# Four token-major projection blocks of 256 columns joined into two pairs of 512

## The chip, the cores and the metric

The kernel runs on one core of a Trainium2 chip. The metric is the device time of one execution in microseconds (us), as the median of several runs. The profile comes from one further execution of the same program.

## The reference, cut to what matters

The program is one transformer layer over 512 + 1024 tokens of width 1024, in fp32. The part at issue is the input projection and what consumes it:

```
u    = rmsnorm(x) * g                      # 1536 tokens x 1024
proj = u @ w_in + b_in                     # split by columns:
       na_q, na_k, na_v   512 each         # neighbourhood attention
       gla_q, gla_k       256 each         # gated linear attention (GLA)
       gla_v, gla_g       512 each
       lr_fwd, lr_bwd      16 each         # decay gates of the GLA
       gate_na, gate_gla 1024 each
gla  = bidirectional scan(gla_q, gla_k, gla_v, decay), normed, * silu(gla_g)
```

The kernel keeps each fp32 operand as a high and a low part and forms a product from three matmuls: high by high, high by low, low by high. A "split" makes the two parts: ScalarE (ACT) copies with rounding to the high part, VectorE (DVE) subtracts it from the source for the low part.

## The kernel before, in words

The token operand (`u_hi`, `u_lo`) stays in SBUF. The projection runs as a list of units. **Channel-major units** (`dense_cm`, line 211) hold a weight tile of 128 columns stationary and stream 512 tokens: 8 steps of three matmuls of 512 columns (lines 225 to 227). **Token-major units** (`dense_tm`, line 255, with `tm_half`, line 244) hold 128 tokens stationary and stream a weight block of 256 columns: 8 steps of three matmuls of 256 columns (lines 250 to 252). There are six token-major blocks of 256 columns: 0 and 1 are `gla_v`, 2 and 3 `na_v`, 4 and 5 `gla_g`. Block 0 is done earlier with the gate columns; the middle stage does the others, twelve token tiles each, the last two tiles together in one unit.

The order of the middle stage is the list `mid` (line 815): block 4, the channel-major `k1`, blocks 1, 5, 2, 3, then eight channel-major `na` tiles and eight gate units. `run_dense` (line 343) walks this list. Each step yields a cost (0.325 for a token-major step, 0.65 for a channel-major one), and when the summed cost passes 3.9 the generator `gla_all` (line 554) issues its next piece. So the GLA is laid between the projection's matmuls by hand, every 12 steps of 256 columns or every 6 of 512. Engines run their instructions in the order in which they are issued.

The GLA treats 512 tokens at a time in eight **levels**. A level is a group of score matmuls on PE (line 622), then on DVE `ew` (line 625) for the next level's operands and `merge`, which copies the scores out of PSUM (on ACT for the last two levels). Two PSUM banks hold scores, so the next score group waits for the merges of this one. After the last segment of a sequence come an update of the states, three pieces of `scan` (line 710: 24 DVE operations for the longer sequence) and the outputs (`out_mm`, line 718), which need the finished scan.

Evictions: when a token tile is done, `out_tm` (line 313) is issued within the next two steps. DVE adds the bias into a staging tile `st` (two buffers). Blocks 4 and 5 then go through ACT (Silu) and GpSimd and a store. Blocks 2 and 3 are split by ACT and DVE into a tile `svr` or `svl` (one buffer each, by turns) and stored by two DMAs. All DMAs here are issued by SyncE (SP) in order.

Weights pass a ring (`Ring`, line 32): two raw buffers, and three pairs of high and low, each with its own fixed place; all are 128 x 1024. An item is half a 256-column block, or one channel-major tile. PSUM gives three banks to projection results.

Of the kernel before, what the change touches and what calls it, by code (L numbers as in the profile page):

```python
# [31 lines left out]
class Ring:  # L32


    def __init__(self, nc, raw, rawtag, nraw, pool, tag, nslots, items):
        self.nc, self.raw, self.pool, self.items = nc, raw, pool, items
        self.rawtag, self.tag, self.nraw, self.nslots = rawtag, tag, nraw, nslots
        self.loaded, self.parts = [], []

    def load(self):  # L40
        i = len(self.loaded)
        t = self.raw.tile([128, 1024], F32, tag=self.rawtag, bufs=self.nraw, name=f"{self.tag}r{i}")
        self.nc.sync.dma_start(t, self.items[i])
        self.loaded.append(t)

    def split(self):
        i = len(self.parts)
        t = self.loaded[i]
        hi = self.pool.tile([128, 1024], F32R, tag=self.tag + "h", bufs=self.nslots, name=f"{self.tag}h{i}")
        lo = self.pool.tile([128, 1024], F32R, tag=self.tag + "l", bufs=self.nslots, name=f"{self.tag}l{i}")  # L50
        self.nc.scalar.activation(hi, t, AF.Copy)  # L51
        self.nc.vector.tensor_tensor(lo, t, hi.bitcast(F32), op=ALU.subtract)  # L52
        self.parts.append((hi, lo))

    def fill(self, live):

        n = len(self.items)
        while True:
            if len(self.loaded) < n and len(self.loaded) - len(self.parts) < self.nraw:
                self.load()  # L60
            elif len(self.parts) < len(self.loaded) and len(self.parts) - live < self.nslots:
                self.split()
            else:
                return

    def step(self, live):

        if len(self.parts) < min(len(self.items), live + self.nslots):
            if len(self.loaded) == len(self.parts):
                self.load()  # L70
            self.split()
            if len(self.loaded) < len(self.items):
                self.load()

    def get(self, i):
        return self.parts[i]
# [3 lines left out]
def tile_trunk(ctx: ExitStack, tc: tile.TileContext, d: dict, y: bass.AP):  # L80
    nc = tc.nc
# [25 lines left out]
    rngp = rnge.enter_context(tc.tile_pool(name="rng", bufs=1))  # L107
# [22 lines left out]
    def add_mv(b):  # L130
        add(f"mv{b}", d["wmv"][2 * b], d["wmv"][2 * b + 1])
# [17 lines left out]
    ring = Ring(nc, raw, "wraw", 2, rngp, "w", 3, items)  # L149
# [8 lines left out]
    zero = cst.tile([128, 128], F32, name="zero")  # L158
    V.memset(zero, 0.0)
# [78 lines left out]
    TM = (0, 4, 1, 5, 2, 3)  # L238

    def load_brow(b):  # L240
        brow[b] = stg2.tile([128, 256], F32, tag="brow", name=f"brow{b}")
# [13 lines left out]
    def dense_tm(b, i, evac):  # L255
# [4 lines left out]
        def mm():  # L260
            if i == 0:
                ring.fill(wi)
            if b not in brow:
                load_brow(b)
            if i == 6 and TM.index(b) < 5:
                load_brow(TM[TM.index(b) + 1])
# [11 lines left out]
        return mm  # L278

# [33 lines left out]
    def out_tm(p, b, i):  # L313
# [108 lines left out]
    def norm_side():  # L422
# [11 lines left out]
        gkw = p0.tile([128, 512], F32, name="gkw")  # L434
# [30 lines left out]
        for i in range(1, 12):  # L465
# [6 lines left out]
            if i == 4:  # L472
                SP.dma_start(gkw, d["gkw"])
                load_brow(4)
                SP.dma_start(gng, d["gng"])
# [10 lines left out]
    ns = norm_side()  # L486
    warm = ps("b")
# [1366 lines left out]
```

## Time and profile before

| | |
|---|---|
| median of 3 runs | 2114.01 us (2112.49 to 2114.92) |
| profiled execution, its own time | 2115.74 us |
| its span, first to last instruction | 2114.1 us |
| PE (TensorE matmuls) busy | 2097.4 us, 99% |
| DVE busy | 1320.2 us, 62% |
| ACT busy | 974.5 us, 46% |
| granted TensorE clock, mean | 0.998 |

The span is the first instruction's start to the last one's end. Matmuls overlap one another, so the busy time of PE says only that it had work; its pace is the distance between two starts. "PEclk" is the granted clock as a share of 2.4 GHz.

### The profile page before, as it was taken

How to read it: one execution, taken by the hardware profiler on the slowest of the kernel's cores; microseconds unless marked ns; L12 is line 12 of the kernel's file. 1: busy time of each engine (PE TensorE's matmuls, PEld its weight loads, DVE VectorE, ACT ScalarE, POOL GpSimd, SP SyncE). 2: the span in 40 equal slices, each digit the busy share in tenths (PEclk: the TensorE clock that was granted, in tenths of full speed). 3: DMA queues.
4: the chain of work that ended last, by engine and by line, in shares of the span. 5: the costliest groups of instructions: out<-in, count | busy, mean ns of one | idle time of the engine just before them, and what ended most of it. 6: DMA issues, size and time to landing. Idle time of an engine off the chain costs nothing.

```text
span 2114.1 us, 32007 instructions
## 1 busy us (share of the span) xinstructions
PE 2097.4 (99%) x11964; PEld 1890.3 (89%) x11964; DVE 1320.2 (62%) x2428; ACT 974.5 (46%) x1914; POOL 66.8 (3%) x92
## 2 busy tenths in 40 slices
PE   9999999999999999999999999999999999999998
PEld 8899998887888888898898999999999888888887
DVE  6465885767346666465476777997887444443543
ACT  6532232333345555452353666676666333233442
POOL 1020200000000000000000000000000000000000
PEclk9999999999999999999999999999999999999999
DMA  6342334464376776466666566766876755454643
GB/s 210 115 151 83 97 112 143 122 168 92 110 243 201 222 213 202 148 212 227 239 219 248 175 162 174 227 202 197 264 236 176 261 200 188 155 169 165 219 170 110
DMA packets 256426, 381.86 MB, mean 181 GB/s; under 512 B 35856, under 2 KB 163856, under 8 KB 256272
## 3 DMA queue, kind: packets, MB, share of 16 engines
q1 hardware_dynamic: 256128, 379.56, 57.4%
q8 instruction: 94, 1.54, 0.3%
q14 instruction: 60, 0.49, 0.1%
q10 hardware_dynamic: 144, 0.26, 0.0%
HBM read 256.02 MB, written 123.73 MB: 180 GB/s over the span
## 4 chain that ended last, share of the span: by engine, by line
PE 81%; DVE 2%; DMA 1%; ACT 1%; issue 1%; POOLq 0%; SPq 0%; DVEq 0%; ACTq 0%
PE psd L225 6%; PE psd L227 6%; PE psd L226 6%; PE psa L1416 4%; PE psa L1417 4%; PE psa L1418 4%; PE psa L1571 2%; PE psa L1572 2%; PE psa L1570 2%; PE psb L1571 2%; PE psb L1570 2%; PE psb L1572 2%; PE psc L1571 2%; PE psc L1572 2%; PE psc L1570 2%; PE psc L976 2%
## 5 line engine op out<-in xcount | busy, mean ns | idle before, releaser
L154 DVE TENSOR_TENSOR al<-al,ah 128x1024 fp32r<-128x1024 f32 x82 | 100.2, 1223 | 146.4 <-ACT ah L153 139.2
L153 ACT ACTIVATE ah<-al 128x1024 fp32r<-128x1024 f32 x82 | 86.6, 1058 | 226.3 <-DMA al<-ads 134.3
L225 PE MATMUL psd<-uhiS,wh 128*128 128x512 f32 x448 | 180.3, 402 | 0.8 <-ACT st L287 0.8
L227 PE MATMUL psd<-uhiS,wl 128*128 128x512 f32 x448 | 175.4, 391 | 0.0
L226 PE MATMUL psd<-uloS,wh 128*128 128x512 f32 x448 | 174.9, 390 | 0.0
L1416 PE MATMUL psa<-c,uwh 128*128 128x384 f32 x512 | 171.8, 335 | 1.4 <-ACT xa L1363 0.8
L1417 PE MATMUL psa<-c,uwh 128*128 128x384 f32 x512 | 171.1, 334 | 0.1
L1418 PE MATMUL psa<-c,uwl 128*128 128x384 f32 x512 | 171.0, 334 | 0.0
L1321 DVE TENSOR_TENSOR uwl<-ux,uwh 128x512 fp32r<-128x512 f32 x192 | 131.1, 687 | 59.3 <-ACT uwh L1337 58.4
L52 DVE TENSOR_TENSOR wl<-wr,wh 128x1024 fp32r<-128x1024 f32 x70 | 85.5, 1223 | 115.0 <-ACT wh L51 104.1
L1337 ACT ACTIVATE uwh<-ux 128x512 fp32r<-128x512 f32 x192 | 119.9, 625 | 80.1 <-DVE ux L1331 66.7
L51 ACT ACTIVATE wh<-wr 128x1024 fp32r<-128x1024 f32 x70 | 73.8, 1055 | 146.6 <-PE psc L1221 66.0
L225 PEld LDWEIGHTS psd<-uhiS,wh 128*128 128x128 f32 x448 | 84.2, 188 | 19.2 <-ACT st L287 1.2
L227 PEld LDWEIGHTS psd<-uhiS,wl 128*128 128x128 f32 x448 | 84.1, 188 | 18.3
L226 PEld LDWEIGHTS psd<-uloS,wh 128*128 128x128 f32 x448 | 84.3, 188 | 16.0
L1416 PEld LDWEIGHTS psa<-c,uwh 128*128 128x128 f32 x512 | 96.1, 188 | 2.1 <-ACT xa L1363 1.1
L1417 PEld LDWEIGHTS psa<-c,uwh 128*128 128x128 f32 x512 | 96.1, 188 | 0.5 <-DVE c L1271 0.4
L1418 PEld LDWEIGHTS psa<-c,uwl 128*128 128x128 f32 x512 | 96.1, 188 | 0.0
L250 PE MATMUL psd<-wh,uhiS 128*128 128x256 f32 x320 | 93.2, 291 | 0.0
L225 PE MATMUL psd<-uhiP,wh 128*128 128x512 f32 x224 | 90.8, 405 | 0.0
L251 PE MATMUL psd<-wl,uhiS 128*128 128x256 f32 x320 | 90.8, 284 | 0.0
L252 PE MATMUL psd<-wh,uloS 128*128 128x256 f32 x320 | 90.7, 283 | 0.0
(547 smaller groups left out, 5897.7 us busy)
## 6 DMA issues: line engine op xcount, KB each, us to landing
ux<-in_wup_dram SPq DMA_DIRECT2D x64, 512.0 KB
al<-ads SPq DMA_DIRECT2D x48, 512.0 KB
al<-ad SPq DMA_DIRECT2D x34, 512.0 KB
bq<-t_d SPq DMA_DIRECT2D x64, 256.0 KB
wr<-in_wst_dram SPq DMA_DIRECT2D x28, 512.0 KB
gate_d<-st SPq DMA_DIRECT2D x48, 256.0 KB
sg<-gate_d SPq DMA_DIRECT2D x32, 384.0 KB
ad<-xa SPq DMA_DIRECT2D x64, 192.0 KB
```

Of the source, the lines that this page charges most:

```text
L154: V.tensor_tensor(lo, src, hi.bitcast(F32), op=ALU.subtract)
L225: T.matmul(p, wh, xh[:, k, sl], start=(k == 0), stop=False)
L226: T.matmul(p, wh, xl[:, k, sl], start=False, stop=False)
L227: T.matmul(p, wl, xh[:, k, sl], start=False, stop=(k == 7))
L1321: V.tensor_tensor(lo, usrc.pop(m - 1), hi.bitcast(F32), op=ALU.subtract)
L1337: A.activation(uhl[m][0], usrc[m], AF.Copy)
L1416: T.matmul(u[b], wh[:, es], c[:, 0, k], start=(new and k == 0), stop=False, skip_group_check=True)
L1417: T.matmul(u[b], wh[:, es], c[:, 1, k], start=False, stop=False, skip_group_check=True)
L1418: T.matmul(u[b], wl[:, es], c[:, 0, k], start=False, stop=(k == 3), skip_group_check=True)
L1570: T.matmul(p, ah[:, jj], bh[:, cs], start=((new or last) and jj == 0), stop=False, skip_group_check=True)
L1571: T.matmul(p, ah[:, jj], bl[:, cs], start=False, stop=False, skip_group_check=True)
L1572: T.matmul(p, al[:, jj], bh[:, cs], start=False, stop=(kh == 1 and jj == 7), skip_group_check=True)
```

## The change

The blocks (4, 5) and (2, 3) become two pairs. A pair has one weight tile for each of its 8 steps, `[128, 1024]`, high part in the left 512 columns and low part in the right; a step is three matmuls of 512 columns, and a pair needs 8 steps for a token tile where its two blocks needed 16 of half the width. The first unit takes token tiles 0 and 1 together, the last one 10 and 11. The weights of a pair come as eight raw tiles of 128 x 512, loaded into the tiles `svr` and `svl`, two at a time. The ring's eight buffers of 128 x 1024 serve raw, high or low as they come free, and also hold the eight tiles of a pair. `k1` is moved to the front, block 1 to the end. Pair 0's weights are split during `k1`, pair 1's during pair 0's last unit, block 1's during pair 1's last unit.

```diff
 class Ring:
-    def __init__(self, nc, raw, rawtag, nraw, pool, tag, nslots, items):
...
+    def __init__(self, nc, pool, nbuf, items):
+        self.nc, self.pool, self.items = nc, pool, items
+        self.free, self.limit, self.done = list(range(nbuf)), len(items), 0
         self.loaded, self.parts = [], []
+    def alloc(self, dt, name):
+        s = self.free.pop(0)
+        return s, self.pool.tile([128, 1024], dt, tag=f"w{s}", name=name)
...
+    def release(self, live):
+        while self.done < min(live, len(self.parts)):
+            self.free += self.parts[self.done][:2]
+            self.done += 1
...
-    for n in ("q0", "k0", "q1"):
+    for n in ("q0", "k0", "q1", "k1"):
         add(n, d["wst"][ST[n]])
-    add_mv(4)
-    add("k1", d["wst"][3])
-    add_mv(1)
-    add_mv(5)
-    add_mv(2)
-    add_mv(3)
+    add("mv1", d["wmv"][0], d["wmv"][1])
...
-    ring = Ring(nc, raw, "wraw", 2, rngp, "w", 3, items)
+    ring = Ring(nc, raw, 8, items)
+    ring.limit = where["mv1"]
-    zero = cst.tile([128, 128], F32, name="zero")
-    V.memset(zero, 0.0)
...
+    PAIRS = ((4, 5), (2, 3))
+    pw = [dict(n=0, raw=[], parts={}) for _ in PAIRS]
+    def pw_step(q, split=True):
+        w = pw[q]
+        if split and w["raw"] and ring.free:
+            k = len(w["parts"])
+            t = w["raw"].pop(0)
+            s, x = ring.alloc(F32R, f"pw{q}{k}")
+            split_act(x[:, :512], x[:, 512:], t)
+            w["parts"][k] = s, x
+        while w["n"] < 8 and len(w["raw"]) < 2:
+            t = stg2.tile([128, 512], F32, tag=("svr", "svl")[w["n"] % 2], bufs=1, name=f"pr{q}{w['n']}")
+            SP.dma_start(t, d["wpr"][q, w["n"]])
+            w["raw"].append(t)
+            w["n"] += 1
+    def pw_ahead(mm, q):
+        def run():
+            for n, cost in enumerate(mm()):
+                yield cost
+                if n % 3 == 2:
+                    pw_step(q)
+        return run
+    def dense_pair(q, i, evac, nxt=None):
+        def step(p, k, j):
+            x = pw[q]["parts"][k][1]
+            xh, xl = tok_ap(u_hi, k, j), tok_ap(u_lo, k, j)
+            T.matmul(p, xh, x[:, :512], start=(k == 0), stop=False)
+            T.matmul(p, xh, x[:, 512:], start=False, stop=False)
+            T.matmul(p, xl, x[:, :512], start=False, stop=(k == 7))
+        def end(p, j):
+            for e in range(2):
+                evac(p[:, e * 256:e * 256 + 256], PAIRS[q][e], j)
+        def mm():
+            if i == 0 and q == 0:
+                ring.release(where["k1"] + 1)
+            if i == 9 and nxt:
+                nxt(-1)
+            ii = (i, i + 1) if i in (0, 10) else (i,)
+            p = {}
+            for k in range(8):
+                for _ in range(2):
+                    if k not in pw[q]["parts"]:
+                        pw_step(q)
+                for j in ii:
+                    if k == 0:
+                        if j == 1:
+                            flush()
+                        p[j] = ps("d")
+                    step(p[j], k, j)
+                    yield 0.68
+                    if k == 7:
+                        done.append(lambda j=j: end(p[j], j))
+                if i == 0:
+                    pw_step(q)
...
+                if i == 10:
+                    ring.free.append(pw[q]["parts"][k][0])
+                    if nxt:
+                        nxt(k)
+        return mm
+    def next_pair(k):
+        pw_step(1, k >= 0)
+    def next_ring(k):
+        ring.limit = len(items)
+        if k in (0, 1):
+            ring.load()
+        elif k in (3, 5):
+            ring.split()
...
-            r = stg2.tile([128, 4, 2, 64], F32R, tag=("svr", "svl")[i % 2], bufs=1, name=f"svr{uid[0]}")
+            r = stg2.tile([128, 4, 2, 64], F32R, tag=("svr", "svl")[(i + b) % 2], bufs=1, name=f"svr{uid[0]}")
...
-    mid = []
-    mid += [dense_tm(4, i, out_tm) for i in range(12)]
-    for n_, dst, cb in (("k1", glak_d, 3),):
-        mid += [dense_cm(n_, seg, out_cm(dst, cb, 128, cb < 2)) for seg in range(3)]
-    for b in (1, 5, 2, 3):
-        mid += [dense_tm(b, i, out_tm) for i in range(12)]
+    mid = [pw_ahead(dense_cm("k1", seg, out_cm(glak_d, 3, 128)), 0) for seg in range(3)]
+    for q, nxt in enumerate((next_pair, next_ring)):
+        mid += [dense_pair(q, i, out_tm, nxt) for i in (0, *range(2, 11))]
+    mid += [dense_tm(1, i, out_tm) for i in range(12)]
```

The bias rows of a pair are loaded earlier (three buffers in place of two), the zeros for the warm-up matmuls share a buffer with another tile and are written a little later, and the later stages take their weight buffers from the same eight in the same number as before.

## Rows read from the trace of the kernel before

**Rows 1.** By stretch: busy us (instructions) of each engine, then granted clock, DMA share, GB/s.

```profile
core 0: us, PE busy (x) PEld busy (x) DVE busy (x) ACT busy (x) POOL busy (x), PEclk, DMA share, GB/s
112.00:222.00 110.00, 110.00 (x880) 103.02 (x879) 65.83 (x123) 30.90 (x67) 14.67 (x18) 1.00 0.38 121
...
267.00:328.00 61.00, 60.57 (x531) 58.46 (x530) 49.49 (x105) 16.82 (x38) 0.73 (x1) 1.00 0.34 109
...
332.00:336.00 4.00, 4.00 (x21) 3.83 (x20) 1.08 (x3) 0.42 (x1) 0.00 (x0) 0.57 0.20 60
```

**Rows 2.** Line 250: instructions by form, duration ns min/median/max, first and last start.

```profile
L250 PE MATMUL psd<-wh,uhiS x320: 278/283/561, 127.1 to 358.8; 128*128 128x256 f32 x160
...
L250 PE MATMUL psd<-wh,uhiP x160: 277/283/386, 115.6 to 323.8; 128*128 128x256 f32 x160
```

**Rows 3.** Timeline of PE, 256-column products: start, duration, engine, line (56 starts apart).

```profile
204.94 0.28 PE L250 MATMUL psd<-wh,uhiS 128*128 128x256 f32 x1
...
211.66 0.28 PE L252 MATMUL psd<-wh,uloS 128*128 128x256 f32 x1
```

**Rows 4.** Timeline of PE, last stage, 512-column products (31 starts apart).

```profile
1719.84 0.39 PE L1571 MATMUL psa<-bl,ah 128*128 128x512 f32 x1
...
1726.86 0.39 PE L1572 MATMUL psb<-bh,al 128*128 128x512 f32 x1
```

**Rows 5.** Timeline of DVE, block 2: a level begins, the next eviction, the one after.

```profile
277.20 0.69 DVE L633 TENSOR_TENSOR Q0S<-q0S,Y0S 128x512 f32<-128x512 f32 x1
...
281.17 0.41 DVE L316 TENSOR_TENSOR sv<-psd,brow 128x256 f32<-128x256 f32 x1
...
282.46 0.42 DVE L316 TENSOR_TENSOR sv<-psd,brow 128x256 f32<-128x256 f32 x1
```

**Rows 6.** Chain of waits ahead of the long wait of PE: start, duration, what.

```profile
318.63 4.09 DMA nv_d<-svr
...
322.83 0.42 ACT svr L153
```

**Rows 7.** Timeline of PE at that wait; in brackets the idle time and its end.

```profile
331.62 0.46 PE L727 MATMUL psb<-stt0S,qd0S 128*128 128x128 f32 x2 [2.57 <-DVE stt0S L716]
```

**Rows 8.** Chain of waits, 512-column section: two score groups, one level apart.

```profile
369.72 1.09 PE psa L622 x16
...
375.12 0.97 PE psa L622 x13
```

**Rows 9.** Timeline of DVE, block 4: two evictions through the same staging buffer.

```profile
119.53 0.42 DVE L316 TENSOR_TENSOR sv<-psd,brow 128x256 f32<-128x256 f32 x1
...
125.63 0.42 DVE L316 TENSOR_TENSOR sv<-psd,brow 128x256 f32<-128x256 f32 x1 [3.66 <-DMA glag_d<-sv]
```

**Rows 10.** Timeline of SP, same stretch: the store between them.

```profile
121.24 0.32 SPq L335 DMA_DIRECT2D glag_d<-sv  x1
```

**Rows 11.** The page, part 5: splits of 512 elements.

```profile
L1321 DVE TENSOR_TENSOR uwl<-ux,uwh 128x512 fp32r<-128x512 f32 x192 | 131.1, 687 | 59.3 <-ACT uwh L1337 58.4
...
L1337 ACT ACTIVATE uwh<-ux 128x512 fp32r<-128x512 f32 x192 | 119.9, 625 | 80.1 <-DVE ux L1331 66.7
```

**Rows 12.** Timelines of SP and DVE: a 256 KB load, and the instruction that its landing released.

```profile
930.58 0.32 SPq L1072 DMA_DIRECT2D xr<-go_d  x1
...
933.33 1.23 DVE L52 TENSOR_TENSOR wl<-wr,wh 128x1024 fp32r<-128x1024 f32 x1 [0.26 <-DMA xr<-go_d]
```

**Rows 13.** Timelines of SP and ACT: a 512 KB load, and the split that it released.

```profile
62.16 0.33 SPq L43 DMA_DIRECT2D wr<-in_wst_dram  x1
...
65.81 1.06 ACT L51 ACTIVATE wh<-wr 128x1024 fp32r<-128x1024 f32 x1 [6.19 <-DMA wr<-in_wst_dram]
```

**Rows 14.** Timeline of DVE: scaled queries, then the first scan of eight operations.

```profile
308.47 0.68 DVE L683 TENSOR_TENSOR qd0S<-q0S,Y0S 64x512 f32<-64x512 f32 x1
...
319.19 0.34 DVE L715 SCALAR_TENSOR_TENSOR stt0S<-stt0S,cd0S 64x128 f32<-64x128 f32 x1
...
322.22 0.42 DVE L316 TENSOR_TENSOR sv<-psd,brow 128x256 f32<-128x256 f32 x1
```

**Rows 15.** Timeline of PE, first products after the warm-up.

```profile
8.45 1.09 PE L193 MATMUL psa<-ident,xn 128*128 128x128 f32 x8 [1.39 <-DVE xn L185]
```

More of the change, by code (lines that the diff above doesn't have):

```diff
@@ L64, in fill @@
                 return
[L66 to L73, printed above, removed]
     def get(self, i):
-        return self.parts[i]
+        return self.parts[i][2:]
 @with_exitstack
@@ L262, in mm @@
                 ring.fill(wi)
[L263 to L266, printed above, removed]
             if i == 11:
@@ new lines, in pw_ahead @@
+    def pw_ahead(mm, q):
[37 more added lines that the diff above has]
+                    pw_step(q)
+                    if k == 4:
+                        for b in PAIRS[q]:
+                            if b not in brow:
+                                load_brow(b)
+                if i == 6 and k == 0:
+                    load_brow(PAIRS[1][0] if q == 0 else 1)
+                if i == 10:
[3 more added lines that the diff above has]
+        return mm
@@ L433, in norm_side @@
         SP.dma_start(gkb, d["gkb"])
-        gkw = p0.tile([128, 512], F32, name="gkw")
         xn = {}
@@ L472, in norm_side @@
             if i == 4:
+                gkw = p0.tile([128, 512], F32, tag="v0r", bufs=2, name="gkw")
                 SP.dma_start(gkw, d["gkw"])
                 load_brow(4)
+                load_brow(5)
                 SP.dma_start(gng, d["gng"])
@@ L486, in tile_trunk @@
     ns = norm_side()
+    zero = p0.tile([128, 4, 32], F32, tag="lrt", bufs=4, name="zero").rearrange("p a b -> p (a b)")
+    V.memset(zero, 0.0)
     warm = ps("b")
@@ L1224, in wout @@
                         V.tensor_tensor(hs, acc[t], hs, op=ALU.add)
+                ring.release(wi + 1)
                 hook(n * 4 + kq)
@@ L1290, in factors @@
         return out
-    uraw, uhl, useq = {}, {}, []
+    uraw, uhl, useq, uslot = {}, {}, [], {}
     for p in range(33):
@@ L1300, in u_load @@
             for e in es:
-                x = raw.tile([128, 1024], F32, tag="wraw", bufs=2, name=f"ux{p}{e}") if p % 2 == 0 else tmp(f"ux{p}{e}")
+                s, x = ring.alloc(F32, f"ux{p}{e}") if p % 2 == 0 else (None, tmp(f"ux{p}{e}"))
+                uslot.setdefault(p, []).append(s)
                 SP.dma_start(x, d["wup"][p % 16 * 2 + e])
@@ L1324, in u_step @@
                 uraw.pop(p)
+                ring.free += [s for s in uslot.pop(p) if s is not None]
                 u_load(p + 2)
@@ L1333, in u_step @@
             if m % 2 == 0:
-                uhl["t"] = [rngp.tile([128, 1024], F32R, tag=f"w{c}", bufs=3, name=f"uw{c}{m}") for c in "hl"]
+                uslot["w", m + 1], uhl["t"] = zip(*[ring.alloc(F32R, f"uw{c}{m}") for c in "hl"])
             sl = slice(m % 2 * 512, m % 2 * 512 + 512)
@@ L1418, in up_all @@
                         T.matmul(u[b], wl[:, es], c[:, 0, k], start=False, stop=(k == 3), skip_group_check=True)
+                    ring.free += uslot.pop(("w", n), ())
                     ev(pos)
@@ L1778, in _layout @@
     mv = [gv, gv + 256, nav, nav + 256, gg, gg + 256]
-    d["wmv"] = c(np.stack([stat(w[h * 512:(h + 1) * 512, m:m + 256]) for m in mv for h in range(2)]))
+    d["wmv"] = c(np.stack([stat(w[h * 512:(h + 1) * 512, gv + 256:gv + 512]) for h in range(2)]))
+    d["wpr"] = c(np.stack([w[:, m:m + 512].reshape(8, 128, 512) for m in (gg, nav)]))
     v0 = np.concatenate([w[:, gv:gv + 256], w[:, lr:lr + 32]], 1)
```

27 lines of the change are left out of this document (10 added, 17 removed).

## The prediction

> **What bounds the kernel now.** I read the shares of the engines first: PE is busy 99% of the span, so what counts is its pace and the few places where it has nothing to do. The windows by stage come next [rows 1]. From 112 to 222 us PE never rests and DVE is at 60%; from 267 to 328 us, under blocks 2 and 3, DVE is busy 81% of the time and PE loses 0.43 us. Just after comes the longest wait of the middle stage, and in the window behind it the granted clock is 0.57, so part of it is at 1.2 GHz: 4 x 0.43 = 1.7 us lost. Line 250 shows 480 matmuls [rows 2], 96 for each of five blocks; lines 251 and 252 repeat them, so the four joined blocks have 4 x 96 x 3 = 1152. Their start-to-start distance is (211.66 - 204.94)/56 = 0.120 us [rows 3]. For a streamed operand of 512 columns, tokens stationary, the last stage shows (1726.86 - 1719.84)/31 = 0.2265 us [rows 4].
>
> The second bound stands close behind. In block 2 one level occupies DVE from 277.20 to 281.17, 3.97 us, and one eviction 1.29 us, because the subtraction waits in line for ACT's copy [rows 5]. A level of PE is 36 x 0.120 + 1.3 = 5.6 us and holds 1.5 evictions, so DVE needs 3.97 + 1.94 = 5.9: DVE, not PE, sets the pace there. The chain ahead of the long wait says the same: a store of `svr` holds ACT's next copy 4.20 us, from 318.63 to 322.83 [rows 6], the scan stands behind it on DVE, and PE waits 2.57 us for the scan [rows 7].
>
> **What the matmuls give.** 1152 x 0.120 = 138.2 us become 576 x 0.2265 = 130.5: -7.8 us, all on PE. The Trainium skill, "TensorE: Matmul & The Clock Gate", section on the 56 ns gap, has N/2.4 GHz plus about 2.5 ns between warm matmuls; by that the joining would give only about 1.5 us and the kernel would end some 6 us later than I say. The trace does not agree with it: 13 ns, not 2.5, lie on top of 256/2.4 = 107.
>
> **What the shorter time asks of DVE.** Score groups in a 512-column section are 375.12 - 369.72 = 5.40 us apart [rows 8]: six steps of 3 x 0.2265 (4.08) and 1.3. Pairs cost 0.68 a step, so 3.9/0.68 = 5.74 steps, 3.9 us, lie between two pieces: 5.2 us a level. DVE's work per token is unchanged, but the evictions now come in twos, and in fours at the first and last unit of a pair, where two token tiles end one step apart. The staging buffers are still two, `svr` and `svl` one each. A staging buffer of blocks 4 and 5 came back 6.1 us after its eviction (119.53 to 125.63 [rows 9]), 4.39 of them after SP issued the store [rows 10]. Four places follow, with t the start of a score group; the group after the next needs the work of the level between.
>
> *A, tokens 0 and 1 of pair 0.* The third and fourth eviction must wait for the first two buffers. Token 0 ends at t + 3.3; buffers back at t + 9.4 and 9.8; last eviction ends at t + 10.3, the level behind it at t + 14.2. PE wants it at t + 10.4. Wait 3.8.
>
> *B, from pair 0 to pair 1.* Eight splits of 512, about 0.69 each on DVE and 0.63 on ACT [rows 11], must run in the last unit, with only two raw buffers. A 256 KB load took 2.75 us from issue to use [rows 12], a 512 KB one 3.65 [rows 13]; I take 3.2, between the two, since SP also carries stores here. A buffer's round is 3.2 + 0.63 + 0.69 = 4.5. From the unit's start: splits end at 2.7, 4.0, 7.2, 8.5, 11.7; a level's 3.97 stands behind the fifth (15.7); 16.4, 17.1; token 10's evictions 17.9; the eighth split 20.9; token 11's evictions wait for buffers, 17.1 + 6.1 = 23.2, and end at 24.1; the next level at 28.1. PE wants that after 22 steps (15.0) and three pieces of GLA (3.4), at 18.4. Wait 9.7, on PE in several parts.
>
> *C, tokens 0 and 1 of pair 1.* Token 0 ends 8.6 us after the last score group of B; its evictions 9.9 and 11.2. Token 1's first copy waits for `svr`, 9.9 + 4.2 = 14.1, its second for `svl`, 15.4; they end at 16.3, the level behind at 20.3. PE wants it at 3 x 5.2 = 15.7. Wait 4.6.
>
> *D, levels 2 to 5 under the rest of pair 1.* 0.72 token per level, 2 x 1.29 each: DVE needs 3.97 + 1.85 = 5.8 against 5.2. Wait 4 x 0.6 = 2.4.
>
> *E, from pair 1 to block 1.* The scan now falls into the last unit and behind it. Between the state update and the outputs DVE has scaled queries (1.4), two splits of 1024 (2.5, at the 1.23 of [rows 12]), 24 scan operations (3 x 3.03 = 9.1 [rows 14]), four evictions (5.2), a wait for `svr` (4.2 - 1.3 = 2.9) and a light eviction (0.4): 21.4 us. PE has 3.9 x 3.9 = 15.2. Wait 6.2. The same sum for before, 20.6 against 16.8, gives 3.8 where 2.57 was seen, so it is good to about 1 us.
>
> Together 26.7 us of new waits. What goes: the old waits and the slow clock behind them, 0.43 + 2.57 + 1.7 = 4.7. What comes with the new: before, PE had waited 2.57 us ahead of the fall of the clock. B, C and E have waits of that size and A too; PE running slowly lets DVE catch up, so I count three of the four, 3 x 1.7 = 5.1.
>
> **What costs nothing.** k1's place: pair 0's first five splits run under k1's 16 us of matmuls, where ACT is mostly idle (30.9 of 110 us); if late, PE waits a split, 1.3 us. Each pair loads eight times 256 KB in place of four times 512 KB: 8 more issues of 0.32 us on SP, which waits more than it issues. GpSimd's 24 multiplications are the same. The later zeros for the warm-up hide in the 1.39 us that PE waits after it [rows 15]; uncovered, some tenths. Later stages get the same buffers in the same order.
>
> **Sum:** -7.8 - 4.7 + 26.7 + 5.1 = +19.3 us. The profiled execution's own 2115.7 us (span 2114.1) becomes 2135.0; it stands 1.7 us above the median, which becomes 2114.0 + 19.3 = 2133.3.
>
> **Rivals.**
> *Faster, the buffers come back in time.* If staging and raw buffers return within about 2 us, the queue of DVE alone counts: A and B fit, C keeps 2.0, D 0.4 (the before, too, lost only 0.43), E 18.5 - 15.2 = 3.3. Then -7.8 - 4.7 + 5.7 = -6.8: 2107 us. For it speaks the 512-column section, where PE keeps 5.40; against it both returns of over 4 us. 0.17.
> *Half the waits.* Returns of some 2.2 us and loads of 1.6: A 1.7, B 4.2, C 2.6, D 1.4, E 4.2, one slow clock: +3.3, 2117 us. 0.13. By the Trainium skill, "DMA: Bandwidth & Descriptors", section on the anatomy of one DMA (there for DMAs that GpSimd issues), a transfer takes 2.0 us plus its bytes over 436 GB/s, 2.3 us for these stores, which would be this case; the rows, with SP issuing, show 4.2 and 4.4.
> *More.* Loads of 3.65, four slow clocks, E's store issues in a row before the return counts, k1's cover gone: +5 to +8, about 2140 us. 0.20.
> *The pair's matmuls are not faster than two halves.* Nothing gained, 2141 us; rows 4 have the same shape of operands. 0.02.
>
> **The numbers.** My forecast has 0.48 and the price of a load or a return moves it between 2124 and 2138. A measurement of this kernel tells about 0.2% (4.2 us) from no change. Faster by more: the first rival and a little of the second, 0.18. Within: part of the second and the forecast's edge, 0.08. Slower: 0.74. The range leaves out the first rival and the top: 2110 to 2149.
>
> **What would show it.** Right: 576 starts 0.227 apart; PE waits for DVE merges (line 660), or for the eviction's bias addition, at the four places; DVE waits of 3 to 4 us ended by stores of `sv` and `svr`; windows with a clock below 1; the scan wait longer than 2.57. Wrong: score groups 5.2 us apart through both pairs, or evictions of token 1 that wait for no store.

## The result and the profile after

| | before | after |
|---|---|---|
| median of the runs | 2114.21 us | 2152.34 us (2152.24 to 2153.85) |
| ratio, 95% interval | | 1.0182 (1.017 to 1.0194) |
| profiled execution, own time / span | 2115.74 / 2114.1 us | 2152.37 / 2150.6 us |
| granted clock, mean | 0.998 | 0.990 |

Slower by 38.1 us; the forecast was 19.3, the range ended at 2149. From the page of the kernel after:

```profile
span 2150.6 us, 30885 instructions
PE 2105.2 (98%) x11388; PEld 1868.8 (87%) x11388; DVE 1320.4 (61%) x2436; ACT 976.2 (45%) x1922; POOL 64.7 (3%) x92
...
PEclk9999899999999999999999999999999999999999
```

DVE and ACT have the same work as before, to 2 us. To see where the time went, each distance between two starts of matmuls is taken apart: PE's idle time, half of the rest where the granted clock is at its lower level (1.2 of 2.4 GHz), and what is left, PE's streaming at full clock. Summed over the span:

| us | before | after | difference |
|---|---|---|---|
| PE idle | 9.2 | 37.9 | +28.7 |
| lost at the lower clock | 3.4 | 15.3 | +11.9 |
| streaming | 2093.7 | 2089.7 | -4.1 |

The sum, +36.5, is the difference of the spans. The stretch at the lower clock in the first 30 us, ahead of the middle stage, differs from trace to trace: 1.7 us of before's 3.4 stand there, none of after's 15.3. From 420 us on the two kernels idle alike; the loss lies in the middle stage. This is what PE waits for from 100 to 420 us (engine, bank and line of the matmul, then the releaser; total, times, longest), to be read against [rows 7]:

```profile
PE psa L694 <- DVE att0S L732: 16.0, 4, 5.4
PE psd L239 <- DVE sv L385: 6.4, 1, 6.4
PE psa L694 <- DVE att0P L732: 4.4, 1, 4.4
PE psd L240 <- DVE wl L54: 2.5, 1, 2.5
PE psa L683 <- issue: 1.9, 1, 1.9
```

Lines 694 and 732 are the scores and the merge (622 and 660 of before), 239 and 240 block 1's matmuls, 385 the eviction's bias addition, 683 the first level of GLA. The matmuls ahead of the waits start at 130.3 (1.87 us), 154.6 (4.44: place A), 225.4 and 237.9 (5.41 and 4.87: B), 261.4 (5.32: C), 341.9 and 350.3 (2.48 and 6.40: E); D lost 1.4 in small pieces. Behind each large one PE ran at the lower clock. The windows behind A, both waits of B, C and E, in the columns of [rows 1]:

```profile
160.00:166.00 6.00, 5.97 (x29) 4.96 (x30) 5.93 (x11) 0.75 (x2) 1.25 (x2) 0.72 0.00 0
...
230.00:235.00 5.00, 3.77 (x19) 3.24 (x20) 3.62 (x7) 1.38 (x3) 1.13 (x2) 0.50 0.83 260
...
243.00:250.00 7.00, 6.89 (x28) 5.71 (x29) 6.87 (x14) 0.00 (x0) 0.00 (x0) 0.57 0.02 7
...
266.00:273.00 7.00, 5.93 (x24) 4.92 (x25) 5.55 (x11) 2.78 (x9) 0.00 (x0) 0.51 0.07 23
...
355.00:362.00 7.00, 5.00 (x24) 5.03 (x25) 5.67 (x17) 0.83 (x2) 0.00 (x0) 0.52 0.50 145
```

Between them PE keeps its pace. Two starts from the timeline of PE, fifteen matmuls apart (other lines left out):

```profile
301.12 0.39 PE L298 MATMUL psd<-pw,uhiS 128*128 128x512 f32 x1
...
304.54 0.39 PE L298 MATMUL psd<-pw,uhiS 128*128 128x512 f32 x1
```

(304.54 - 301.12)/15 = 0.228 us, as [rows 4] had it. Why PE waits is told by the queues of DVE, ACT and SP (timeline: start, length, engine and line; in brackets the idle time before and what ended it), in the order A (four), C (two), and four at E:

```profile
148.26 0.76 DVE L385 TENSOR_TENSOR sv<-psd,brow 128x256 f32<-128x256 f32 x2 [0.92 <-PE psd L299]
...
148.76 1.28 ACT L401 ACT_TABLE_LOAD   x1 [7.98 <-DVE sv L385]
...
151.35 6.39 SPq L404 DMA_DIRECT2D glag_d<-sv  x4
...
154.15 0.93 DVE L385 TENSOR_TENSOR sv<-psd,brow 128x256 f32<-128x256 f32 x2 [5.13 <-DMA glag_d<-sv]
...
261.54 0.42 ACT L145 ACTIVATE svr<-sv 128x256 fp32r<-128x256 f32 x1 [4.27 <-DMA nv_d<-svr]
262.78 0.42 ACT L145 ACTIVATE svr<-sv 128x256 fp32r<-128x256 f32 x1 [0.82 <-DVE sv L385]
...
348.52 7.06 SPq L47 DMA_DIRECT2D wr<-in_wst_dram  x3
...
352.91 1.06 ACT L53 ACTIVATE wh<-wr 128x1024 fp32r<-128x1024 f32 x1 [6.24 <-DMA wr<-in_wst_dram]
...
354.00 1.23 DVE L54 TENSOR_TENSOR wl<-wr,wh 128x1024 fp32r<-128x1024 f32 x1 [6.87 <-ACT wh L53]
...
357.68 0.34 DVE L787 SCALAR_TENSOR_TENSOR stt0S<-stt0S,cd0S 64x128 f32<-64x128 f32 x1
```

At A, DVE stands 5.13 us before a bias addition, for a store that must give a staging buffer back; the next level is behind it in DVE's queue. At C, ACT stands for a store of `svr` (the trace gives the tiles `svr` and `svl` this one name). It is the tile filled last: an eviction takes `svr` or `svl` by `(i + b) % 2`, so the last eviction of a token and the first of the next one share a tile. At E, na0's weights are loaded and split at once: DVE stands 6.87 us before that split, ahead of the third and the fourth eviction and the scan. For B, the chain that ended last, from 216 us on (start, length, what; a DMA from its issue):

```profile
217.13 2.67 DMA pr<-in_wpr_dram
...
220.55 0.70 DVE pw L146
221.27 5.11 DMA pr<-in_wpr_dram
...
226.46 0.64 ACT pw L145
...
227.12 0.70 DVE pw L146
...
258.55 2.83 DMA nv_d<-svr
```

The first raw load takes 2.67 us, the third 5.11: 3 us before it the 1 MB of `v0S` went out. The last line is at C: the store that ACT waits for.

### The profile page after: what moved, and what is told of

It is laid out like the page before. It is cut to its first block, busy times and chain, and to the rows that moved or that the text cites. A ratio compares the mean times of both kernels' runs of the same rounds, so it can differ in the third digit from the quotient of the medians.

```text
span 2150.6 us, 30885 instructions
## 1 busy us (share of the span) xinstructions
PE 2105.2 (98%) x11388; PEld 1868.8 (87%) x11388; DVE 1320.4 (61%) x2436; ACT 976.2 (45%) x1922; POOL 64.7 (3%) x92
## 4 chain that ended last, share of the span: by engine, by line
PE 86%; DVE 5%; DMA 3%; issue 3%; ACT 2%; POOL 1%; SPq 0%; POOLq 0%; ACTq 0%; DVEq 0%
PE psd L215 7%; PE psd L217 7%; PE psd L216 7%; PE psa L1489 4%; PE psa L1490 4%; PE psa L1491 4%; PE psa L1646 2%; PE psa L1644 2%; PE psa L1645 2%; PE psb L1644 2%; PE psb L1646 2%; PE psb L1645 2%; PE psc L1646 2%; PE psc L1644 2%; PE psc L1645 2%
## 5 line engine op out<-in xcount | busy, mean ns | idle before, releaser
L54 DVE TENSOR_TENSOR wl<-wr,wh 128x1024 fp32r<-128x1024 f32 x62 | 75.8, 1224 | 132.6 <-ACT wh L53 110.3
L53 ACT ACTIVATE wh<-wr 128x1024 fp32r<-128x1024 f32 x62 | 65.3, 1055 | 141.5 <-PE psc L1291 65.0
L217 PE MATMUL psd<-uhiP,wl 128*128 128x512 f32 x224 | 87.7, 392 | 0.0
L216 PE MATMUL psd<-uloP,wh 128*128 128x512 f32 x224 | 87.4, 390 | 0.0
L1491 PE MATMUL psb<-c,uwl 128*128 128x384 f32 x256 | 85.5, 334 | 0.0
```

The lines of the kernel that those rows point to most:

```text
L216: T.matmul(p, wh, xl[:, k, sl], start=False, stop=False)
L217: T.matmul(p, wl, xh[:, k, sl], start=False, stop=(k == 7))
L1491: T.matmul(u[b], wl[:, es], c[:, 0, k], start=False, stop=(k == 3), skip_group_check=True)
```

## The experiments

"Idle" and "slow" are the sums of the table above, for each run's own profile. Each ratio is to the kernel before on the same chip. A profile is one execution: those of x3_fill5, y4_abce and v4_half took 2.8 to 3.5 us more than their medians, and of the slow clock up to 3.3 us lie in the first 30 us (1.7 in x4_half, 3.3 in z3_ring).

| run | median us | ratio, 95% | idle | slow |
|---|---|---|---|---|
| changed kernel | 2152.34 | 1.0182 (1.0170 to 1.0194) | 37.9 | 15.3 |
| x1_pack | 2144.80 | 1.0144 (1.0129 to 1.0159) | 35.4 | 7.8 |
| x2_vlate | 2150.19 | 1.0171 (1.0154 to 1.0188) | 35.0 | 15.2 |
| x3_fill5 | 2148.43 | 1.0163 (1.0148 to 1.0178) | 35.9 | 15.3 |
| x5_rawq | 2153.73 | 1.0186 (1.0171 to 1.0201) | 36.9 | 18.5 |
| x4_half | 2153.11 | 1.0184 (1.0169 to 1.0199) | 35.5 | 11.8 |
| y1_abc | 2134.59 | 1.0098 (1.0083 to 1.0113) | 25.6 | 8.8 |
| y2_fill | 2150.47 | 1.0174 (1.0159 to 1.0189) | 24.0 | 10.8 |
| y4_abce | 2129.78 | 1.0072 (1.0055 to 1.0089) | 21.2 | 13.4 |
| z1_single | 2141.50 | 1.0127 (1.0112 to 1.0142) | 30.8 | 13.7 |
| z2_order | 2132.21 | 1.0081 (1.0064 to 1.0097) | 23.8 | 10.1 |
| z3_ring | 2118.62 | 1.0022 (1.0012 to 1.0031) | 11.3 | 5.0 |
| z5_lazy | 2129.48 | 1.0067 (1.0050 to 1.0084) | 21.8 | 6.4 |
| v1_inpl | 2149.32 | 1.0165 (1.0148 to 1.0181) | 36.7 | 14.2 |
| v2_best | 2129.71 | 1.0073 (1.0056 to 1.0090) | 21.5 | 6.4 |
| v3_binpl | 2114.50 | 1.0002 (0.9993 to 1.0012) | 8.7 | 3.3 |
| v4_half | 2131.68 | 1.0086 (1.0071 to 1.0101) | 22.1 | 8.3 |
| v5_early | 2122.06 | 1.0036 (1.0023 to 1.0049) | 16.9 | 5.0 |
| v6_wide | 2129.95 | 1.0071 (1.0054 to 1.0088) | 23.4 | 7.8 |

### One place at a time

**x1_pack**, place A: a token's two evictions share a staging buffer.

```diff
-        t = stg.tile([128, 512], F32, tag="st", ...)[:, :256]
+            if b % 2 == 0:
+                both[i] = stg.tile([128, 512], F32, tag="st", ...)
+            t = both[i][:, b % 2 * 256:b % 2 * 256 + 256]
```

> The two evictions of a token share one staging buffer of 512 columns (each takes its half), so two buffers hold the four evictions of tokens 0 and 1 and none has to wait for a store. Theory 'buffers' (PE waits because DVE stands in line behind a store that must bring a buffer back): the wait of 4.44 us at 154.6 falls under 0.5, the slow stretch behind it (1.7 us lost) goes, and the last part of the wait at 237.9 shrinks by about 1.3 (the DVE wait for glag_d at 238.0): 6 to 8 us in all, 2144 to 2146. Theory 'DVE work' (levels and evictions fill DVE, and a buffer more only moves the wait): within 1 us of the changed kernel, 2151 to 2153.

2144.8, 7.5 less than the changed kernel: "buffers". A is gone from PE's waits (L701 is line 694 of before this edit), B is 9.4 in place of 10.3; E's longest wait grew by 1.2. Of the gain only 2.5 us is idle time; slow clock fell by 7.5, where the theory counted 1.7, so that its size is in part luck:

```profile
PE psa L701 <- DVE att0S L739: 15.8, 4, 6.2
PE psd L239 <- DVE sv L392: 7.6, 1, 7.6
```

**x2_vlate** and **x5_rawq**, place B: the 1 MB load out of the way, or four raw buffers more.

```diff
-            SP.dma_start(x["v"][:, :n], glav_d[...])
+            x["vload"] = lambda: SP.dma_start(x["v"][:, :n], glav_d[...])
...
+                if l == 5 and si == 0:
+                    x["vload"]()
```

> The 1 MB load of v for each unit of GLA moves from the unit's start to its level 5. Theory 'queue' (the third and fourth raw load of pair 1 land 5.1 us after their issue because the 1 MB of v0S went out 3 us before them): they land in about 2.75 us as the first two did, the wait of 5.41 at 225.4 falls to about 3, with perhaps half of the slow stretch behind it: 2 to 4 us in all, 2148 to 2150. Theory 'raw buffers alone' (5 us is what a round of load and split costs here): the load's place changes nothing, 2152.

```diff
-        while w["n"] < 8 and len(w["raw"]) < 2:
-            t = stg2.tile(...)
+        while w["n"] < 8 and (len(w["raw"]) < 2 or spare):
+            t = spare.pop(0) if spare else stg2.tile(...)
```

> Pair 1's raw loads 2 to 5 go to four quarters of the tile qd of 0S, which nothing uses until the end of its first segment, so six raw buffers are there in place of two. Theory 'buffers': loads no longer wait for a split, the two waits of 5.41 and 4.87 us from pair 0 to pair 1 fall together to 3 to 5 (the 1 MB of v0S still goes out ahead of these loads), and one of the two slow stretches (3.4 lost each) goes: 7 to 11 us, 2141 to 2145. Theory 'DVE work': the levels that stand between the splits are what PE waits for, and less than 2 us is gained: 2150 to 2152.

x2_vlate: ACT has the third raw load 2.66 us after its issue (220.51 to 223.17), the wait at 225 falls from 5.41 to 2.86, and 2.2 us go: "queue". x5_rawq: the loads leave earlier, at 219.2, and land at the same time, behind the 1 MB; B is 9.4 and the end does not move. So depth alone was not what B lacked. SP and ACT in x2_vlate, then in x5_rawq:

```profile
220.51 0.98 SPq L279 DMA_DIRECT2D pr<-in_wpr_dram  x2
...
223.17 0.63 ACT L145 ACTIVATE pw<-pr 128x512 fp32r<-128x512 f32 x1 [2.76 <-DMA pr<-in_wpr_dram]
```

```profile
219.20 3.38 SPq L279 DMA_DIRECT2D qd0S<-in_wpr_dram  x4
...
226.73 1.99 ACT L145 ACTIVATE pw<-qd0S 128x512 fp32r<-128x512 f32 x3 [4.92 <-DMA qd0S<-in_wpr_dram]
```

**x3_fill5**, place E: block 1 asks for the next stage's weights later.

```diff
-            if i == 0:
+            if i == 5:
                 ring.fill(wi)
```

> Block 1 asks for the next stage's weights in its unit 5 and not in its unit 0. Theory 'third split': na0's load, issued at 348.5, and its split (ACT 352.9, DVE 354.0) stand ahead of the fourth eviction and of the scan; without them there, the wait of 6.40 at 350.3 falls under 1 and the slow stretch behind it (3.4 lost) mostly goes: 7 to 9 us, 2143 to 2145. Theory 'scan and evictions' (my forecast's sum for E: 21.4 us of DVE work against 15.2 of PE, with two splits): the wait only loses the 1.23 us of one split, about 2 us in all, 2150.

2148.4, 3.9 less: between the two expectations. The 6.40 at 350 became 1.77 + 1.09 + 1.04 and its slow stretch went, so the third split was there; but a wait of 1.65 with a new slow stretch came up at 488, where GLA's next sequence meets stores of `nkS_d`. At what stays of E, ACT waits for a store of `svr` ahead of the scan, as I forecast. That this store makes the rest is not shown: no run takes it away with the third split gone.

```profile
351.59 0.42 ACT L145 ACTIVATE svr<-sv 128x256 fp32r<-128x256 f32 x1 [4.42 <-DMA nv_d<-svr]
```

**z1_single**: the first unit of a pair undone.

```diff
-            ii = (i, i + 1) if i in (0, 10) else (i,)
+            ii = (i, i + 1) if i == 10 else (i,)
...
-        mid += [dense_pair(q, i, out_tm, nxt) for i in (0, *range(2, 11))]
+        mid += [dense_pair(q, i, out_tm, nxt) for i in range(11)]
```

> The first unit of each pair takes one token, not tokens 0 and 1 together; nothing else is changed. Theory 'four at once' (the four evictions that end together, not the amount of work, made the waits at 154.6 and 261.4): both fall under 1 us with the slow stretches behind them (1.7 and 3.4); pair 1's first unit has half the matmuls beside its last splits, so the wait from pair 0 to pair 1 may grow by up to 3: 9 to 13 us below the changed kernel, 2139 to 2143. Theory 'DVE pace' (DVE's work per token is the same, so its waits come back a level later): 2149 or more.

2141.5, 10.8 less, by a reordering alone. A is 0.4 us and C is gone; B is 8.8, and a wait of 1.8 us came at 280. So the number of evictions that end together made them, not DVE's work per token.

**v1_inpl**: a second way to end C.

```diff
-            r = stg2.tile([128, 4, 2, 64], F32R, tag=("svr", "svl")[(i + b) % 2], ...)
-            split_act(r[:, :, 0], r[:, :, 1], t3)
+            r = t        # t: one of st, st, svr, svl by turns, bias addition into t[:, :, 1]
+            split_act(r[:, :, 0].bitcast(F32R), r[:, :, 1].bitcast(F32R), r[:, :, 1])
```

> On the changed kernel, evictions of blocks 2 and 3 use one buffer of 512 columns each and not two of 256 and 512 (the bias addition writes into the lo half, ACT writes the hi half, DVE subtracts in place), from four that take turns: the two of st, svr and svl. Instructions stay. Theory 'buffers': tokens 0 and 1 of pair 1 have a buffer each, so the wait of 5.32 at 261.4 falls under 1.5 and the slow stretch (3.4) goes, and the fourth eviction at block 1 no longer waits for a store: 7 to 11 us below the changed kernel, 2141 to 2145. Theory 'DVE work': the same work, the wait comes back a level later: 2149 or more.

C fell from 5.32 to 1.81 and its slow stretch went, but the end moved by 3.0 only. C went as "buffers" had it, nearly; the time, 2149.3, is one that "DVE work" had. 1.3 us of wait appeared at 488 again, 0.7 more at 358 and 0.5 more at 288. **v3_binpl** is the same edit on the kernel before.

> The kernel before the change with the one-buffer evictions of blocks 2 and 3. Theory 'buffers': its waits of 0.43 and 2.57 us and the slow stretch behind them (1.7), which follow ACT's wait of 4.20 us for a store of svr, go: 3 to 5 us faster than before, 2109 to 2111. Theory 'DVE work' (the scan is late for its own length): within 1.5 us of before.

No difference. Its one wait is what it was (2.57 in [rows 7]; lines 727 and 716 there):

```profile
PE psb L731 <- DVE stt0S L720: 2.6, 1, 2.6
```

So the store of `svr` that ACT waits for in [rows 6] did not make the scan late.

### Together

**y1_abc** joins x1, x2 and x5 and gives token 1 of pair 1 hi/lo buffers of its own; **y4_abce** adds a change at E (the last two parts of the diff):

```diff
-            r = stg2.tile([128, 4, 2, 64], F32R, ...)
+            r = keep[b % 2]... if i == 1 else stg2.tile([128, 4, 2, 64], F32R, ...)
...
-            if i == 0:
+            if i == 2:
                 ring.fill(wi)
...
-        if k in (0, 1):
+        if k in (0, 1, 6):
             ring.load()
```

> The shared staging buffer, the late load of v and the raw loads in qd together, and token 1 of pair 1 takes two quarters of the same tile for its hi/lo pieces, so that its copies wait for no store. Theory 'buffers and queue': no wait at 154.6; from pair 0 to pair 1 one wait of about 2.5 in place of 5.41 and 4.87; at 261 under 1 in place of 5.32; one slow stretch left of the four behind them: 2128 to 2132. Theory 'DVE work': what these buffers free is taken by the levels behind them, the waits of tokens 0 and 1 come back one or two levels later, and it stays above 2140.

> As y1_abc, and na0's load goes out at step 6 of pair 1's last unit and its split at block 1's unit 2 (in the changed kernel both at unit 0). Theory 'third split': of 2.48 + 6.40 + 0.34 us at block 1 some 5 stay (the split of mv1's second half and a store return of svr ahead of the scan) and one slow stretch of the two goes: 7 to 9 us below y1_abc, 2120 to 2124. Theory 'scan and evictions': 2 to 3 us below y1_abc.

2134.6 and 2129.8: 17.8 and 22.6 us back; y1_abc lies between its two theories, and so does the step from it to y4_abce. B keeps 1.19 + 0.77 + 3.51 in y1_abc, C 2.06; E gave 4.8.

**y2_fill**: is it the clock?

```diff
+                keep_busy({"0P04": 17, "0S02": 21, "0S03": 19, "0S06": 21}.get(f"{w}{l}", 0))
                 res = diag(qk) if l == 0 else scores(*nq)
```

> 17, 21, 19 and 21 matmuls of 512 columns that nobody reads stand ahead of the four score groups that wait longest (154.6, 225.4, 237.9, 261.4), so PE is busy for some 0.5 us less than each wait and no buffer or order changes. Theory 'clock on its own' (the slow stretches follow from PE's idleness and cost 1.7 + 3.4 + 3.4 + 3.4 = 11.9 us in the changed kernel): the granted clock stays at full in these four places and 8 to 12 us go, 2140 to 2144. Theory 'catch-up' (what PE loses at half clock DVE uses to catch up, so that it is lost in the next wait otherwise): the stretches go, the waits behind them grow by nearly as much, 2148 to 2152.

2150.5. The clock stays up at A, the second wait of B and C:

```profile
154.00:166.00 12.00, 11.05 (x60) 8.53 (x60) 11.32 (x20) 1.59 (x4) 3.21 (x3) 1.00 0.10 33
225.00:236.00 11.00, 7.94 (x40) 6.08 (x39) 6.43 (x12) 2.89 (x6) 1.34 (x2) 0.87 0.44 149
240.00:250.00 10.00, 10.00 (x67) 7.86 (x65) 9.79 (x18) 0.00 (x0) 0.10 (x1) 1.00 0.11 35
264.00:274.00 10.00, 9.28 (x60) 7.47 (x61) 8.19 (x18) 5.13 (x15) 0.00 (x0) 1.00 0.10 33
```

From 140 to 280 us 9.7 us of slow clock became 1.6, but idle and filling matmuls together are 21.7 where 20.2 were idle, another 1.3 of wait and 1.7 of slow clock came at 288, and 1.1 at 490. The end gained 1.9: "catch-up" by the time, though what came back came as waits, filling and slow clock elsewhere. At these places DVE sets the end, and a slow PE costs little beside it.

**x4_half** and **v4_half**: is the joining worth anything? (Two accumulations of a token take turns in one PSUM bank here, which changes what the four blocks hold; the work is the same.)

```diff
-            T.matmul(p, xh, x[:, :512], start=(k == 0), stop=False)
...
+            for c in (0, 256):
+                T.matmul(p[:, c:c + 256], xh, x[:, c:c + 256], ...)
...
```

> Each matmul of 512 columns of the two pairs is issued as two of 256, so 1152 in place of 576; units, loads, splits and evictions stay. Theory 'pace on the path' (the joining gives what its streaming time says, 5.9 us by the starts of the dense lines, 7.8 by my forecast): 6 to 8 us slower than the changed kernel, 2158 to 2160, with the waits unchanged. Theory 'covered' (in the pairs DVE sets the pace, so PE's longer time only shortens its waits): at most 2 us slower, 2152 to 2154, and the waits shorter by as much as the matmuls are longer.

Streaming grew by 5.8, as it should; idle fell by 2.4 and slow clock by 3.5, and the end moved by 0.8: "covered", though the waits alone took up less than half of it.

```profile
PE psa L696 <- DVE att0S L734: 14.3, 4, 5.5
...
PE psa L696 <- DVE att0P L734: 3.5, 1, 3.5
```

**z3_ring**: the ring under the old blocks in the old order. The eviction's choice of tile is that of the changed kernel too, `(i + b) % 2` in place of `i % 2`.

```diff
+    mid = [dense_tm(4, i, out_tm) for i in range(12)]
+    mid += [dense_cm("k1", seg, out_cm(glak_d, 3, 128)) for seg in range(3)]
+    for b in (1, 5, 2, 3):
+        mid += [dense_tm(b, i, out_tm) for i in range(12)]
```

> The new ring of eight buffers alone, with the five blocks of 256 columns and the order of units as before the change. Theory 'no part of it': 2112 to 2117, no different from before, with the one wait of 2.57 us and its slow stretch. Theory 'shared buffers' (loads and hi/lo parts that take any free buffer start later than with fixed ones): waits for splits at block starts, 2119 or more.

4.4 us slower than before, between the two expectations. One wait is new, of 3.4 us at 324, where block 3 begins. ACT stands 5.58 us for a store of `svr` that left SP behind a load of 512 KB (z3_ring, ACT and SP):

```profile
317.63 0.42 ACT L152 ACTIVATE svr<-sv 128x256 fp32r<-128x256 f32 x1 [1.68 <-issue]
323.63 0.42 ACT L152 ACTIVATE svr<-sv 128x256 fp32r<-128x256 f32 x1 [5.58 <-DMA nv_d<-svr]
...
317.25 0.33 SPq L47 DMA_DIRECT2D wr<-in_wst_dram  x1
318.54 11.48 SPq L411 DMA_DIRECT2D nv_d<-svr  x6
```

The kernel before has the same load and store there, and its eviction at that point does not wait (ACT and SP):

```profile
318.39 0.42 ACT L153 ACTIVATE svr<-sv 128x256 fp32r<-128x256 f32 x1 [0.88 <-DVE sv L316]
...
316.71 0.33 SPq L43 DMA_DIRECT2D wr<-in_wst_dram  x1
```

The difference is the tile. Block 2's last eviction (i = 11) and block 3's first (i = 0) take `svl` and `svr` by `i % 2`, and `svl` twice by `(i + b) % 2`. So by the trace and the diff the wait is not the ring's: at the eviction before it (317.63 for 317.10) z3_ring is 0.5 us late, and of its 4.4 about 1 is left for the ring. No run has the ring with the old choice.

### Towards a version that keeps the joining

**z2_order** puts block 1 between the pairs and takes single first units. (Tokens 3 and 5 of pair 1 write where the second segment of 0S also does, so part of that sequence's output differs.) **z5_lazy** takes that overlap out and lets `fill` split only what an earlier call loaded.

```diff
+    mid += [dense_pair(0, i, out_tm, next_block) for i in range(11)]
+    mid += [pw_ahead(dense_tm(1, i, out_tm), 1) for i in range(12)]
+    mid += [dense_pair(1, i, out_tm, next_ring) for i in range(11)]
```

```diff
+        here = max(len(self.loaded), live + 1)
...
-            elif len(self.parts) < len(self.loaded) and ...
+            elif len(self.parts) < min(here, len(self.loaded)) and ...
```

> An attempt to keep the joined blocks without the stalls: the shared staging buffer, the late load of v, the raw loads in qd and hi/lo pieces of every second token there (as y1_abc), single first units, and block 1 between the two pairs, so that pair 1 is split bit by bit under block 1, pair 1's evictions fall beside the scan and the outputs of 0S, and only na0's one split follows pair 1. Theory 'places' (the time over that of before comes from a few places where splits and evictions meet): 1.9 us at the start of GLA, some 2.5 at the start of block 1, under 1 us in each other place, 3 to 5 us of slow clock: 2112 to 2120. Theory 'DVE pace' (levels 5.2 us apart are too close for DVE): above 2126.

> As z2_order, but the ring never splits a weight whose load goes out in the same call (the split waits for the next call), pair 0's first four raw loads go out together to the tile that 0P uses later, and only token 1 of pair 1 puts its hi/lo pieces there. Theory 'places': the waits of 7.53 us at 375.0 and 1.82 at 363.0 (na2's load of 370.2 and its split of 374.7 and 375.7 ahead of a level) go with the slow stretches behind them (1.7 and 5.1), and at the start of GLA 1.64 + 0.66 + 0.22 shrink to about 1: 2114 to 2119. Theory 'DVE pace': DVE is only late elsewhere, above 2124.

2132.2 and 2129.5: misses. The places of the old order were gone or under 2 us, but what comes after pair 1 was not: 7.53 us at 375 in the first, and in the second 5.03 there and 3.44 ahead of the scan's outputs. **v2_best** is z5_lazy with v1's evictions and na1's load at step 7; **v5_early** has both loads at steps 0 and 1 and their splits at 5 and 7; **v6_wide** is v5_early with steps counted as 0.63. The diff is v5_early's, against z5_lazy:

```diff
-        if k in (0, 2):
+        if k in (0, 1):
             ring.load()
-        elif k == 6:
+        elif k in (5, 7):
             ring.split()
```

> z5_lazy with these one-buffer evictions, and na1's load goes out at step 7 and not at step 2 of pair 1's last unit (it stood beside a load of glag_d that the outputs wait for, 6.5 us). Theory 'buffers': of z5_lazy's 3.44 us at 326, 1.85 at 363 and 5.03 at 373 some 3 in all stay, and two of the three slow stretches (1.7 + 3.4) go: 2116 to 2121. Theory 'DVE work': 2126 or more.

> v2_best with each matmul of 512 columns of the pairs issued as two of 256, as in x4_half. Theory 'path' (with the waits mended PE sets the pace, and the joining is worth its streaming time): 4 to 6 us slower than v2_best. Theory 'covered' (DVE still sets the pace in the pairs): at most 2 us slower.

> v2_best with both loads of the next stage's weights at steps 0 and 1 of pair 1's last unit and their splits at steps 5 and 7, so that no split stands right behind its own load. Theory 'load ahead of split': v2_best's 7.90 us at 370 fall under 1.5 and 1.83 at 358 under 1, with most of the slow clock behind them (1.7 + 5.1): 2116 to 2121. Theory 'DVE work' (evictions and levels are late there anyway): 2125 or more.

> v5_early with a step of the pairs counted as 0.63 in place of 0.68 for the placing of GLA's pieces, so that its levels stand some 0.3 us further apart in the pairs and GLA ends about 12 us later in the same stage. Theory 'DVE pace': the waits ahead of score groups (1.6, 1.2 and the smaller ones) go, 2 to 5 us below v5_early. Theory 'places' (buffers and loads, not pace): within 1.5 us of v5_early.

v2_best: 3.44 became 0.6, but the load that I had moved to the end stood right ahead of its split (SP, ACT, DVE), and PE waited 7.90 us; the time is one that "DVE work" had, by another cause:

```profile
365.30 1.39 SPq L47 DMA_DIRECT2D wr<-in_wst_dram  x3
...
370.25 1.06 ACT L53 ACTIVATE wh<-wr 128x1024 fp32r<-128x1024 f32 x1 [6.79 <-DMA wr<-in_wst_dram]
...
371.34 1.22 DVE L54 TENSOR_TENSOR wl<-wr,wh 128x1024 fp32r<-128x1024 f32 x1 [7.42 <-ACT wh L53]
```

v4_half is 2.0 us above it, at the edge of "covered". Its trace shows no covering: streaming +3.8, but idle +0.6 and slow clock +1.9. v5_early gained 7.6, nearly what "load ahead of split" had. Its waits, each at most 1.8 us:

```profile
PE psa L716 <- DVE att0S L754: 3.9, 3, 1.6
PE psa L716 <- DVE att1P L754: 2.3, 2, 1.3
PE psd L218 <- DVE wl L54: 1.8, 1, 1.8
```

v6_wide, with more room for DVE, was 7.9 slower, which neither theory had: other work met (2.51 and 2.62 us in block 1, 1.96 and 2.14 at 378 and 386). More room between the levels did not help by itself; which pieces of work meet decided more. At 2122.06 v5_early has 30.3 of the 38.1 us back and is still 0.36% above the kernel before. No version here beats it.

## Why the prediction was wrong

**Term by term.** Against the +19.3 of the sum stand the spans' +36.5: streaming gave 4.1 in place of 7.8, idle time grew by 28.7 in place of 23.7 (26.7 new less 3.0 old), slow clock by 11.9 in place of 3.4 (5.1 less 1.7). The mechanism was right in the main, DVE late where buffers are short; its sizes were not, and at B and E a part of the wait had a cause that the sum lacks.

**Right.** Slower; 576 starts 0.23 apart; waits at the four places, for the merges or the bias addition. A 4.4 (forecast 3.8), C 5.3 (4.6), with stores and late evictions as the cause: x1_pack and z1_single end A, z1_single ends C and v1_inpl brings it to 1.8. D 1.4 (2.4). That A and C come so near is partly luck. I had a store's return at 4.4 and 4.2 us after its issue; here it was 2.8 (151.35 to 154.15) and 3.0 (258.55 to 261.54). At A the rest of the round was longer, 3.1 us from the eviction to the store, with a table load of 1.28 on ACT in it, where [rows 9] and [rows 10] have 1.7. At C I misread my own diff: token 1's first copy waits for `svl`, filled last, not for `svr`, and the second copy for no store. A return was thus nearer to the 2.2 us of the rival "Half the waits" than to mine, and the waits still came.

**"I count three of the four, 3 x 1.7 = 5.1."** The largest term that failed: 15.3 us of slow clock, of which the wait at 130 has 1.6, A 1.7, B 5.0, C 2.9 and E 4.0. A stretch behind a wait of about 5 us cost more than the one that I had seen behind 2.57. The remark that a slow PE lets DVE catch up fits y2_fill: of the 8.1 us of slow clock taken away, 3.9 come back as idle or filling time and 1.7 as slow clock at another place. So I read waits and slow clock as one loss, and should have sized it by how late DVE is at each place, not as a wait and an extra.

**E, "two splits of 1024".** 9.2 for 6.2. There is a third split, of na0, whose load is issued in the same call (x3_fill5, y4_abce). The pair's eight tiles fill the ring until its last unit, and I had put only two loads there; a third can go out at its step 6 (y4_abce). With the third split out, 1.77 + 1.09 + 1.04 and the 2.48 before them make 6.4. That this meets the forecast does not show its terms: the sum has a wait for `svr`, which in the changed kernel's trace does not appear at E.

**B, "a buffer's round is 3.2 + 0.63 + 0.69".** 10.3 for 9.7, near by luck: 3.0 of it has another cause. The third and fourth load took 5.1 us behind the 1 MB of `v0S`, which I had not looked for in the queue; without it B is 7.3 (x2_vlate). Raw buffers alone leave 9.4 (x5_rawq), the shared staging buffer alone 9.4 (x1_pack), all three together 5.5 (y1_abc). What each has in the rest was not separated.

**"What costs nothing."** k1's place cost 2.1 us and 1.6 of slow clock at the first level, by the trace: the product of queries and keys (line 669) stands on DVE behind a split that waits for a raw load. No run moved k1 back. The ring, which I priced at nothing, has about 1 us of z3_ring's 4.4 by its trace; the rest is the choice of tile, which my sum does not have at all. ACT and DVE of the changed kernel, at the first level:

```profile
129.87 0.63 ACT L145 ACTIVATE pw<-pr 128x512 fp32r<-128x512 f32 x1 [2.47 <-DMA pr<-in_wpr_dram]
...
131.14 0.69 DVE L669 TENSOR_TENSOR qk<-q0P,k0P 128x512 f32<-128x512 f32 x1
```

**"What the matmuls give", -7.8.** 5.8 us of streaming by x4_half, 3.8 by v4_half; in the runs with the same matmuls the streaming time lies between 2088.0 and 2092.0, so these are good to some 2 us. The rule of the Trainium skill that I weighed ("TensorE: Matmul & The Clock Gate", section on the 56 ns gap) would have given 1.5, by my estimate; the trace speaks against it here too. But the end had 0.8 of it. A gain on PE counts where PE is the one that is late, and in the pairs it was DVE.

**The old wait.** I read ACT's wait for `svr` [rows 6] as what made the scan late [rows 7]. v3_binpl takes it away and the scan is as late. The sum for E that I checked against it agreed by chance or for another reason; that stays open.

What also stays open: v5_early's 7.9 us over before. Its trace has 7.7 us more of idle time, in waits of at most 1.8; no run says which part of the change they come from. The new order of units with the old blocks, and a version without the ring, were not tried.

## What to carry to other kernels

A wider block must be paid in buffers: here it took all eight, nothing could be fetched ahead until a pair's last unit, and splits then stood right behind their loads in two in-order queues. Before joining instructions for PE's sake, look which engine is late in that stage and undo the joining once, alone: it tells the gain at the end, not on the engine. When work that ends together needs more buffers than there are, first let less end together (z1_single: 10.8 us by a reordering); and do not issue a split in the call that issues its load (v5_early against v2_best: 7.6 us). When a run is to test one part of a change alone, compare its diff with the kernel before line by line: z3_ring carried a second part along, and it made most of the difference.

## What the runs showed of the hardware

- Transfers that SP issued behind a large one came later, loads and stores alike. A load of 256 KB was in use 5.2 us after its issue behind 1 MB (221.27 to 226.46), 2.7 us without it (x2_vlate, which moved the 1 MB). For the store it is a comparison of places: `svr` came back 4.2 us after the issue in the kernel before [rows 6], where a load of 512 KB had gone out 1.9 us earlier (316.71), and 3.0 us at C, with no load just ahead. My price of 4.4, too, came from a store [rows 10] that left 1.6 us behind a load of 512 KB (issued at 119.64). I had taken one price for all. For DMAs that GpSimd issues the Trainium skill, "DMA: Bandwidth & Descriptors", section on the anatomy of one DMA, has 2.0 us plus the bytes over 436 GB/s, an estimate of 2.3 us for 128 KB. On SP's queue the store at C took 2.83 by the chain.
- Removing one wait moved others by microseconds more than 100 us later (the 1.65 us at 488 in x3_fill5 and 1.3 in v1_inpl). So places do not add up. Less came than a place had: v1_inpl took 3.5 us of wait and 2.9 of slow clock from C, and the end gained 3.0. More came together than alone: x1_pack, x2_vlate and x5_rawq gave 7.5, 2.2 and -1.4, and y1_abc, which joins them and mends C, 17.8.
